# Attention queries and keys transposed in 32x32 blocks on VectorE during retention and placed through DRAM, instead of on TensorE during attention

## The chip, the cores and the metric

One Trainium2 chip, one of its cores. The metric is the device time of one execution in microseconds (us). The kernel before was run three times: 586.6, 587.24 and 587.29 us, median 587.24.

## What is computed

One layer of a trunk over 1,040 tokens (16 meta tokens and 1,024 others) of width 1,024, in fp32. A normalised input is projected once and cut into three groups: a gated short convolution, an attention with eight heads whose queries and keys come from small latents, and a retention with four heads. Their outputs are concatenated, projected and added to the input. The part that the change touches:

```python
q = (rms_norm(c_q, q_a_norm) @ w_uq).reshape(B, L, MLA_HEADS, QK_HEAD)      # 8 heads of 96 = 64 + 32
kv = (rms_norm(c_kv, kv_a_norm) @ w_ukv).reshape(B, L, MLA_HEADS, QK_NOPE + V_HEAD)
k = jnp.concatenate([k_nope, k_r], axis=-1)
q = rms_norm(q, q_norm)
k = rms_norm(k, k_norm)
q = jnp.concatenate([q[..., :QK_NOPE], apply_rope(q[..., QK_NOPE:], cos, sin)], axis=-1)
k = jnp.concatenate([k[..., :QK_NOPE], apply_rope(k[..., QK_NOPE:], cos, sin)], axis=-1)
s = jnp.einsum('bqhd,bkhd->bhqk', qb, k).astype(jnp.float32) * scale
s = jnp.where(mask[None, None], s, neg)          # blocks of 64 tokens, causal by block
p = jax.nn.softmax(s, axis=-1).astype(v.dtype)
return jnp.einsum('bhqk,bkhd->bqhd', p, v)
```

## The kernel before

Tokens are worked in eight tiles of 128 (`t` = 0 to 7) and one of the 16 meta tokens (`t` = 8). Nearly every matmul operand is kept as two parts, hi and lo, whose sum is the fp32 value, and a product is three matmuls (`mm3`, L112): hi with hi, hi with lo, lo with hi. `split` (L100 to L107) makes the parts: ScalarE rounds to hi, VectorE or GpSimd subtracts for lo.

The stages, in order:
- to about 60 us: inputs arrive; the gate of the attention group.
- to about 130 us: the attention's latents, queries, keys and values (`a_proj`, `a_lat`, `a_up`). Each token tile's queries and keys go to DRAM as q_s and k_s, tokens on rows (L368, L388).
- to about 256 us: retention, in two units `u` of two heads. For each token tile `r_proj` (L420) makes 24 matmuls; the steps behind it are put off by `later` and run one tile step on: `r_rope` rotates on VectorE (rt to qk, L441 to L444) and transposes on TensorE (L453); `r_score` makes the decayed product (qs, L472), `r_out` the output (rop, L487), `r_norm` and `fin` the rest (yp, L511).
- to about 355 us: the convolution, 128 channels at a time, cv, cz and cb being its matmul blocks. Its last quarter runs beside the first scores.
- to 540 us: the attention, head by head (`score`, `p_t`, `attend`), with the early part of the output projection (`partial`) as filling.
- the rest: the output projection.

`load_pair` (L535) reads k and q of a pair of heads back from DRAM, 128 tokens on the partitions. `qk_t` (L655) transposes them on TensorE, four blocks of 128x96 in a group, and splits the result out of PSUM into qT and kT, which the scores read; the weights of the query and key norm (wqk) are multiplied in at this split:

```python
def qk_t(h, g, which):                      # L655: head, half of the tokens, 0 = q, 1 = k
    tp = pst("tq", f"{'qk'[which]}Tp{h}_{g}")
    for j in range(4):
        nc.tensor.transpose(out=tp[:96, j * P:j * P + P], in_=src[:, 4 * g + j, cs], identity=ident)
    if which == 0:
        split(qT[h % 2][0][:96, gs], qT[h % 2][1][:96, gs], tp[:96], scale=wqk[:96])
    else:
        split(kT[h % 2][0][:96, gs], kT[h % 2][1][:96, gs], tp[:96])
```

A scheduler sets the order of each engine's instructions from the program and its own estimates; on the chip that order is fixed, and an engine that waits holds back all that stands behind. SP issues nearly all transfers, in one such queue. Buffers with one tag are shared in turn: hp_pool has two of tag "q" and two of tag "k", and the convolution's ccs, the retention's rwk and the keys share the latter. wp holds weights (12 pairs of hi and lo), wsp three staging tiles for them.

## Time and profile before

| | |
|---|---|
| median of 3 runs | 587.24 us |
| the profiled execution, first to last instruction | 590.4 us (its page gives no time beyond this span) |
| instructions | 9,705 |
| HBM read, written | 48.75 MB, 21.00 MB |
| busy: TensorE, VectorE, ScalarE, GpSimd | 98%, 56%, 42%, 38% |

How to read it: PE is TensorE, PEld its weight load, DVE VectorE, ACT ScalarE, POOL GpSimd, SP the engine that issues transfers. L661 is line 661 of the kernel. In a row `out<-in x8` names what is written, what is read and how many. Matmuls overlap, and the end of one is modelled, so durations of neighbours can't be added; starts can be compared. A row of the waits names who waited, for whom, how long in total, how often, and the longest.

### The profile page before, as it was taken

Reading aid. Unit: us, or ns where it says so; the run is one execution under the profiler, and the core shown is the slowest. Engines: PE = TensorE matmul, PEld = TensorE weight load, DVE = VectorE, ACT = ScalarE, POOL = GpSimd, SP = SyncE. Lnnn points to the kernel's source line nnn. Section 1 sums busy time; section 2 is a strip of 40 time slices with the busy share of each in tenths; the row PEclk is TensorE's granted clock in tenths of the full one; section 3 lists DMA queues with packets and bytes.
Section 4 is the critical chain, followed back from the end, with each engine's and each line's share of the span. In section 5 each row is a group of like instructions: output and inputs, shape, how many; then the busy total and the mean of one; then the engine's idle time right before and its main releaser. Section 6 shows DMA issues by size and latency. Waiting matters only on the chain.

```text
span 590.4 us, 9705 instructions
## 1 busy us (share of the span) xinstructions
PE 577.6 (98%) x3465; PEld 482.2 (82%) x3465; DVE 331.6 (56%) x777; ACT 249.3 (42%) x584; POOL 224.1 (38%) x327
## 2 busy tenths in 40 slices
PE   8989899999999999999999999999999999999996
PEld 5867799988777777788889888888888888877885
DVE  5547578888435442483252557766758658564132
ACT  6764445655114321341020327755656556544000
POOL 2023157677203230060430986634434344534000
PEclk9999899999999999999999999999999999999999
DMA  8787613364701300040102548316311223113086
GB/s 328 262 261 241 187 48 116 126 197 178 232 2 47 115 0 19 1 129 32 37 26 69 163 140 263 113 37 179 92 53 54 72 90 120 43 46 135 16 273 228
DMA packets 46656, 70.38 MB, mean 119 GB/s; under 512 B 3792, under 2 KB 21840, under 8 KB 46480
## 3 DMA queue, kind: packets, MB, share of 16 engines
q1 hardware_dynamic: 43008, 63.47, 33.5%
q10 hardware_dynamic: 3600, 6.29, 2.9%
q8 instruction: 27, 0.44, 0.3%
q14 instruction: 21, 0.17, 0.1%
HBM read 48.75 MB, written 21.00 MB: 118 GB/s over the span
## 4 chain that ended last, share of the span: by engine, by line
PE 84%; DMA 10%; DVE 3%; ACT 2%; issue 1%; SPq 0%; DVEq 0%; ACTq 0%
PE r L112 17%; PE S L112 9%; PE cv L112 8%; PE part L112 8%; PE A L112 6%; PE o L758 6%; PE pTp L717 5%; DMA out<-ot 4%; PE cz L112 4%; PE cb L112 4%; PE out L112 3%; PE qps L112 3%; DMA xs<-in_xT 2%; DMA xt<-in_x 2%; PE rsp L471 1%; DMA mz_s<-mzz 1%
## 5 line engine op out<-in xcount | busy, mean ns | idle before, releaser
L695 ACT ACTIVATE pr<-S,smx 128x144 f32<-128x144 f32 (+8 forms) x72 | 50.4, 701 | 27.2 <-DVE smx L686 13.3
L686 DVE TENSOR_REDUCE smx<-S 128x1 f32<-128x144 f32 (+8 forms) x72 | 49.8, 701 | 15.7 <-PE S L112 6.3
L703 POOL TENSOR_SCALAR pm<-pr,smx 128x16 f32<-128x16 f32 x64 | 18.5, 289 | 85.1 <-DVE smx L701 61.1
L704 POOL TENSOR_SCALAR pr<-pr,smx 128x128 f32<-128x128 f32 (+3 forms) x64 | 48.1, 752 | 0.6 <-DVE smx L701 0.6
L717 PE MATMUL pTp<-ident,pr 128*128 128x128 f32 x288 | 45.4, 274 | 0.0
L723 ACT COPY pt<-pTp 128x512 f32<-128x512 f32 (+2 forms) x64 | 31.8, 506 | 26.4 <-PE pTp L717 24.9
L717 PEld LDWEIGHTS pTp<-ident,pr 128*128 128x128 f32 x288 | 35.1, 140 | 5.3 <-issue 0.8
L448 POOL TENSOR_SCALAR kw<-qk,con 128x64 f32<-128x64 f32 (+1 forms) x36 | 14.4, 413 | 64.0 <-DVE qk L444 31.3
L758 PEld LDWEIGHTS o<-pt,v 128*64 128x64 f32 x448 | 26.6, 137 | 12.1 <-issue 4.8
L758 PE MATMUL o<-pt,v 128*64 128x256 f32 (+2 forms) x448 | 36.2, 309 | 0.0
L112 PE MATMUL r<-wh_r,xah 128*128 128x512 f32 (+1 forms) x80 | 30.3, 379 | 0.0
L112 PE MATMUL r<-wh_r,xal 128*128 128x512 f32 (+1 forms) x80 | 30.3, 378 | 0.0
L112 PE MATMUL part<-woh,yh 128*128 128x512 f32 x64 | 30.1, 471 | 0.0
L112 PE MATMUL r<-wl_r,xah 128*128 128x512 f32 (+1 forms) x80 | 30.0, 375 | 0.0
L875 DVE SCALAR_TENSOR_TENSOR ot<-out,xr 128x512 f32<-128x512 f32 (+1 forms) x17 | 11.2, 660 | 32.9 <-DMA out<-ot 17.6
L472 DVE TENSOR_TENSOR qs<-rsp,con 128x128 f32<-128x128 f32 x32 | 8.4, 288 | 31.9 <-PE rsp L471 31.8
L112 PE MATMUL r<-wh_r,xbl 128*128 128x512 f32 x64 | 26.1, 407 | 0.0
L112 PE MATMUL r<-wh_r,xbh 128*128 128x512 f32 x64 | 25.9, 405 | 0.0
L112 PE MATMUL r<-wl_r,xbh 128*128 128x512 f32 x64 | 25.7, 402 | 0.0
L112 PE MATMUL part<-wol,yh 128*128 128x512 f32 x64 | 25.5, 399 | 0.0
L112 PE MATMUL part<-woh,yl 128*128 128x512 f32 x64 | 25.2, 394 | 0.0
L766 DVE TENSOR_TENSOR ym<-o,ym 64x256 f32<-64x256 f32 x32 | 13.5, 420 | 16.7 <-PE o L760 16.2
(293 smaller groups left out, 1723.8 us busy)
## 6 DMA issues: line engine op xcount, KB each, us to landing
xt<-in_x SPq DMA_DIRECT2D x16, 256.0 KB, 4.3
ws_r<-in_win SPq DMA_DIRECT2D x16, 256.0 KB, 3.5
ws_c<-in_win SPq DMA_DIRECT2D x16, 256.0 KB, 3.0
wos<-in_wout SPq DMA_DIRECT2D x16, 256.0 KB, 3.5
xp<-in_x SPq DMA_DIRECT2D x16, 256.0 KB, 2.7
p_s<-xp SPq DMA_DIRECT2D x16, 256.0 KB, 2.0
xr<-p_s SPq DMA_DIRECT2D x15, 256.0 KB, 5.2
out<-ot ACTq DMA_DIRECT2D x15, 256.0 KB, 5.3
```

Of the source, the lines that this page charges most:

```text
L112: nc.tensor.matmul(out, lhsT=x_, rhs=y_, start=first and i == 0, stop=last and i == 2)
L448: nc.gpsimd.tensor_scalar(kw[R, j], qk[R, 2 + j], con[R, kd0 + j:kd0 + j + 1], 1.0, op0=ALU.mult, op1=ALU.mult)
L472: nc.vector.tensor_tensor(qs[:, 2 + j], sp[j][:, :P], DT[:, 2 * u + j], op=ALU.mult)
L686: nc.vector.tensor_reduce(sm[:, i // 2:i // 2 + 1], sp[:, :n, :w], axis=AX.XY, op=ALU.max, negate=True)
L695: e = nc.scalar.activation(pr[:, c0:c1].rearrange("p (b c) -> p b c", b=n), sp, AF.Exp, bias=mx, accum_out=sm[:, 5 + i:6 + i])
L703: nc.gpsimd.tensor_scalar(pm[(2 * h + t // 4) % 2][:, t % 4, :NM], pr[:, nk - NM:nk], sm[:, 9:10], 1.0, op0=ALU.mult, op1=ALU.mult)
L704: nc.gpsimd.tensor_scalar(pr[:, :nk - NM], pr[:, :nk - NM], sm[:, 9:10], 1.0, op0=ALU.mult, op1=ALU.mult)
L717: tr_ = nc.tensor.transpose(out=tp[:, b * P:b * P + P], in_=pr[:, c0:c0 + P], identity=ident)
L723: nc.scalar.copy(pt[:, b0:b0 + nb, tt], src)
L758: nc.tensor.matmul(op[64 * cg:64 * cg + 64, c0:c1], lhsT=lv, rhs=src[:, i_, c_], start=b == 0, stop=False)
L766: nc.vector.tensor_tensor(ys, op[64 * cg:64 * cg + 64, :256].rearrange("p (a c q) -> p a c q", a=2, q=64), ys, op=ALU.mult)
L875: nc.vector.scalar_tensor_tensor(ot, acc[:, c0:c1], 0.5, xt, op0=ALU.mult, op1=ALU.add)
```

## The change

- A new step, `turn`, runs eight times in the retention stage, one for each token-tile step from `u` = 0, `t` = 3 on: for each pair of heads first k, then q. It loads the pair's slice (ts) from k_s or q_s, multiplies the first 64 columns of each query by the norm weights (GpSimd, L527), transposes all 32x32 blocks on VectorE (L528, ts to td), and stores td to a new DRAM array T_s with four transfers of 32 partitions each, so that the array holds 96 rows a head and 1,024 tokens in a permuted order.
- `load_head` reads the 96x1,024 values of one head's k and q from T_s, for heads 0 and 1 after the third quarter of the convolution, later at the first tile of each head for the head after next.
- `qk_t` has no transpose: it splits what was loaded, through a view that undoes the permutation. The lo part of k is made on GpSimd now, that of q stays on VectorE.
- wqk becomes a row of 64 weights on all partitions.

```diff
+    def turn(hp, which):
+        src = hp_pool.tile([P, NT, 192], F32, tag="q", name=f"ts{hp}_{which}")
+        dst = hp_pool.tile([P, 6, NT * 32], F32, tag="q", name=f"td{hp}_{which}")
+        nc.sync.dma_start(src, (q_s, k_s)[which].rearrange("t p c -> p t c")[:, :, hp * 192:hp * 192 + 192])
+        if which == 0:
+            nope = src.rearrange("p t (h d) -> p (t h) d", h=2)[:, :, :64]
+            nc.gpsimd.tensor_tensor(nope, nope, wqk[:, None, :].to_broadcast([P, 2 * NT, 64]), op=ALU.mult)
+        nc.vector.transpose(dst.rearrange("p c (t k) -> p t c k", k=32), src.rearrange("p t (c k) -> p t c k", k=32))
+        to = T_s[which][hp].rearrange("(c f) (i r) -> i f c r", f=32, i=4)
+        for i in range(4):
+            nc.sync.dma_start(to[i], dst[32 * i:32 * i + 32])
+
+    turns = [(hp, w) for hp in range(4) for w in (1, 0)]
     for u in range(2):
         for t in [8] + list(range(NT)):
             r_proj(u, t)
             step()
+            if turns and t != 8 and (u or t >= 3):
+                turn(*turns.pop(0))
...
+    def load_head(h):
+        for which in (1, 0):
+            x = hp_pool.tile([P, 1536], F32, tag="qk"[which], name=f"{'qk'[which]}{h}")[:96, :SEQ]
+            nc.sync.dma_start(x, T_s[which][h // 2, 96 * (h % 2):96 * (h % 2) + 96])
+            raw[h, which] = x.rearrange("p (i t k) -> p t i k", i=4, k=32)
+
     def load_pair(hp):
-        qt = hp_pool.tile([P, NT, 192], F32, tag="q", name=f"q{hp}")
-        kt = hp_pool.tile([P, NT, 192], F32, tag="k", name=f"k{hp}")
...
-        nc.sync.dma_start(kt, k_s.rearrange("t p c -> p t c")[:, :, hp * 192:hp * 192 + 192])
-        nc.sync.dma_start(qt, q_s.rearrange("t p c -> p t c")[:, :, hp * 192:hp * 192 + 192])
...
         def qk_t(h, g, which):
...
-            for j in range(4):
-                nc.tensor.transpose(out=tp[:96, j * P:j * P + P], in_=src[:, 4 * g + j, cs], identity=ident)
-            if which == 0:
-                gs = slice(g * 512, g * 512 + 512)
-                split(qT[h % 2][0][:96, gs], qT[h % 2][1][:96, gs], tp[:96], scale=wqk[:96])
...
+            src = raw[h, which][:, 4 * g:4 * g + 4]
+            o = g * 512 + NM * which
+            dst = [x[:96, o:o + 512].rearrange("p (t i k) -> p t i k", i=4, k=32) for x in (qT, kT)[which][h % 2]]
...
+            split(*dst, src, lo_eng=nc.gpsimd if which else nc.vector)
...
+            if t == 0 and h + 2 < H:
+                load_head(h + 2)
```

The rows below are the orders of the two programs, without the number of each row (a number at the end of a name is a buffer's; the change's lines lie some 2 to 18 further down).

On SP, at the end of the queries and keys, before: the last store of q, one of the loads of v, the last store of k, the loads of the first two pairs' queries, then weights.

```order
L388 DMA q_s_70<-kqo7_1636 128x768
L541 DMA v1_3678<-v_s_72 128x8x128
L368 DMA k_s_71<-kqo7_1636 128x768
L540 DMA q0_3303<-q_s_70 128x8x192
L540 DMA q1_3676<-q_s_70 128x8x192
L118 DMA ws_r17_1930<-in_win 128x512
L118 DMA ws_c00_2471<-in_win 128x512
L118 DMA ws_c01_2477<-in_win 128x512
```

and now:

```order
L370 DMA k_s_71<-kqo7_1638 128x768
L523 DMA ts0_1_1890<-k_s_71 128x8x192
L531 DMA kT_s_74<-td0_1_1891 32x6x256 x4
L523 DMA ts0_0_2006<-q_s_70 128x8x192
L531 DMA qT_s_73<-td0_0_2007 32x6x256 x4
L523 DMA ts1_1_2082<-k_s_71 128x8x192
L531 DMA kT_s_74<-td1_1_2083 32x6x256 x4
L523 DMA ts1_0_2155<-q_s_70 128x8x192
L120 DMA ws_r17_1940<-in_win 128x512
L120 DMA ws_c00_2541<-in_win 128x512
L120 DMA ws_c01_2547<-in_win 128x512
L531 DMA qT_s_73<-td1_0_2156 32x6x256 x2
```

The two loads of queries gave way to turns: each is a load and four stores, and the weight loads r17, c00 and c01 stand behind the fourth turn's load.

On VectorE, around the rotation of tile 5 of the first retention unit (qk0_5), before:

```order
L472 TENSOR_TENSOR qs0_3_1884<-rsp0_3_0_1964,con_105 128x128
L472 TENSOR_TENSOR qs0_3_1884<-rsp0_3_1_1965,con_105 128x128
L482 SCALAR_TENSOR_TENSOR state0_1574<-state0_1574,con_105,rup0_3_1972 64x64 x2
L441 TENSOR_TENSOR qk0_5_2048<-rt0_5_2046,con_105 128x256
L442 TENSOR_TENSOR qk0_5_2048<-rt0_5_2046,con_105 128x4x32
L443 TENSOR_TENSOR qk0_5_2048<-rt0_5_2046,con_105 128x4x32
L460 SCALAR_TENSOR_TENSOR zsb0_4_1993<-zsb0_4_1993,rt0_5_2046 128x128
L444 TENSOR_TENSOR qk0_5_2048<-qk0_5_2048 128x256
L500 TENSOR_REDUCE so0_3_2026<-rwk0_3_2024 128x8
L501 SCALAR_TENSOR_TENSOR so0_3_2026<-so0_3_2026,con_105 128x8
```

and now:

```order
L474 TENSOR_TENSOR qs0_3_1886<-rsp0_3_1_1975,con_107 128x128
L446 TENSOR_TENSOR qk0_4_1989<-qk0_4_1989 128x256
L484 SCALAR_TENSOR_TENSOR state0_1576<-state0_1576,con_107,rup0_3_1982 64x64 x2
L528 STREAM_TRANSPOSE td1_1_2083<-ts1_1_2082 128x8x6x32
L443 TENSOR_TENSOR qk0_5_2067<-rt0_5_2065,con_107 128x256
L444 TENSOR_TENSOR qk0_5_2067<-rt0_5_2065,con_107 128x4x32
L445 TENSOR_TENSOR qk0_5_2067<-rt0_5_2065,con_107 128x4x32
L462 SCALAR_TENSOR_TENSOR zsb0_4_2003<-zsb0_4_2003,rt0_5_2065 128x128
L502 TENSOR_REDUCE so0_3_2045<-rwk0_3_2043 128x8
L446 TENSOR_TENSOR qk0_5_2067<-qk0_5_2067 128x256
L503 SCALAR_TENSOR_TENSOR so0_3_2045<-so0_3_2045,con_107 128x8
```

The third turn's transpose (td1_1) stands between the state of tile 3 and the rotation of tile 5; the rest is in the same order, except that a reduction of the norm (so0_3) comes ahead of the rotation's last addition.

On GpSimd, where the last quarter of the convolution meets the first heads (pm and pr are the normalisations of head 0's probabilities, wol the lo parts of output weights), before:

```order
L104 TENSOR_TENSOR wol7_0_3363<-wos7_0_3364,woh7_0_3362 128x512
L703 TENSOR_SCALAR pm0_3346<-pr0_0_3455,smx0_0_3449 128x16
L704 TENSOR_SCALAR pr0_0_3455<-pr0_0_3455,smx0_0_3449 128x128
L607 TENSOR_SCALAR wos6_1_3601<-wos6_1_3601,vec_76 128x512
L607 TENSOR_SCALAR wos7_1_3605<-wos7_1_3605,vec_76 128x512
L578 TENSOR_TENSOR yv1_1_3460<-yv1_1_3460,z1_1_3461 128x512
```

and now:

```order
L721 TENSOR_SCALAR pm0_3420<-pr0_0_3509,smx0_0_3503 128x16
L722 TENSOR_SCALAR pr0_0_3509<-pr0_0_3509,smx0_0_3503 128x128
L106 TENSOR_TENSOR wol7_0_3437<-wos7_0_3438,woh7_0_3436 128x512
L106 TENSOR_TENSOR kt1l_3399<-k1_3377,kt1h_3398 96x512 x2
L601 TENSOR_TENSOR yv1_1_3514<-yv1_1_3514,z1_1_3515 128x512
L721 TENSOR_SCALAR pm0_3420<-pr0_1_3556,smx0_1_3550 128x16
```

Two subtractions for the keys of head 1 (kt1l) stand ahead of the convolution's product and of the next normalisations; two for head 0 (kt0l) stand some ten rows earlier.

## Rows read from the trace of the kernel before

**Rows 1.** TensorE and the others, busy times of the page:

```profile
PE 577.6 (98%) x3465; PEld 482.2 (82%) x3465; DVE 331.6 (56%) x777; ACT 249.3 (42%) x584; POOL 224.1 (38%) x327
```

**Rows 2.** Waits of TensorE, longest first: who, for whom, total, times, longest:

```profile
PE A L112 <- ACT wh_A L103: 2.5, 1, 2.5
```

**Rows 3.** Windows: us, then busy PE, PEld, DVE, ACT, POOL, PEclk, DMA share, GB/s:

```profile
125.00:256.00 131.00, 131.00 (x698) 103.08 (x696) 65.82 (x197) 43.95 (x105) 42.48 (x58) 1.00 0.26 82
...
400.00:540.00 140.00, 139.95 (x1114) 116.74 (x1113) 92.63 (x226) 79.68 (x191) 62.26 (x109) 1.00 0.27 86
```

**Rows 4.** The tile of transposed keys: duration min/median/max ns, first and last start:

```profile
L661 PE MATMUL kTp<-ident,k x64: 270/272/274, 317.7 to 491.7; 128*96 128x128 f32 x64
```

**Rows 5.** Timeline of TensorE at a group of transposes: start us, us, what:

```profile
392.71 0.60 PE L661 MATMUL qTp<-ident,q 128*96 128x128 f32 x4
...
393.33 0.35 PE L112 MATMUL S<-kt0l,qt0h 104*128 104x400 f32 x1
393.51 0.35 PE L112 MATMUL S<-kt0h,qt0l 104*128 104x400 f32 x1
```

**Rows 6.** Loads of the slices k, then of q, from issue to landing, us:

```profile
DMA to landing us min/median/max: 4.7/5.9/7.1
...
DMA to landing us min/median/max: 6.2/6.5/8.3
```

**Rows 7.** Groups of GpSimd's instructions: busy us, mean ns | idle before:

```profile
L104 POOL TENSOR_TENSOR wol<-wos,woh 128x512 fp32r<-128x512 f32 x16 | 20.4, 1295 | 2.6 <-ACT woh L103 2.5
L703 POOL TENSOR_SCALAR pm<-pr,smx 128x16 f32<-128x16 f32 x64 | 18.5, 289 | 85.1 <-DVE smx L701 61.1
L704 POOL TENSOR_SCALAR pr<-pr,smx 128x128 f32<-128x128 f32 (+3 forms) x64 | 48.1, 752 | 0.6 <-DVE smx L701 0.6
```

**Rows 8.** VectorE's long rows, a group and two lines:

```profile
L104 DVE TENSOR_TENSOR yk<-ym,yq 128x1024 fp32r<-128x1024 f32 x2 | 2.4, 1210 | 0.0
...
L634 DVE CAST qt1h<-msk x1: 678/678/678, 330.9 to 330.9; 8x1024 fp32r<-8x1024 f32 x1
...
L635 DVE CAST kt1h<-msk x1: 1558/1558/1558, 333.0 to 333.0; 8x1044 fp32r<-8x1044 f32 x1
```

**Rows 9.** Timeline of SP's queue, the last store of k: start us, us:

```profile
151.49 0.32 SPq L368 DMA_DIRECT2D k_s<-kqo  x1
```

**Rows 10.** Transfers issued from 147 to 162 us: KB each, median us to landing:

```profile
k_s<-kqo SPq DMA_DIRECT2D x1, 384.0 KB, 3.5
```

**Rows 11.** Timeline of VectorE at the rotation of tile 5, start and end:

```profile
178.81 0.42 DVE L441 TENSOR_TENSOR qk<-rt,con 128x256 f32<-128x256 f32 x1 [3.93 <-ACT rt L435]
...
179.75 0.42 DVE L444 TENSOR_TENSOR qk<-qk 128x256 f32<-128x256 f32 x1
```

**Rows 12.** Timeline of TensorE, the transposes of that rotation:

```profile
184.40 0.38 PE L453 MATMUL rtp<-ident,qk 128*128 128x128 f32 x2
```

**Rows 13.** The projections r of the second unit, tiles 4 to 7:

```profile
L112 PE MATMUL r<-wh_r,xbh x32: 390/394/507, 225.2 to 254.6; 128*128 128x512 f32 x32
```

**Rows 14.** Windows after TensorE's wait for the first projection (columns as in rows 3):

```profile
60.00:62.00 2.00, 1.42 (x6) 1.23 (x7) 1.79 (x3) 1.30 (x3) 0.00 (x0) 0.69 0.87 285
62.00:64.00 2.00, 2.00 (x8) 1.90 (x7) 1.84 (x3) 1.35 (x3) 0.00 (x0) 0.50 0.92 286
```

**Rows 15.** Timeline of GpSimd before the clearing of vr [idle before <- releaser]:

```profile
346.71 0.70 POOL L703 TENSOR_SCALAR pm<-pr,smx 128x16 f32<-128x16 f32 x1 [1.38 <-DVE smx L701]
...
349.98 1.29 POOL L578 TENSOR_TENSOR yv<-yv,z 128x512 f32<-128x512 f32 x1 [0.86 <-DVE smx L701]
...
354.51 0.95 POOL L822 MEMSET vr<- 128x1024 f32 x1
```

**Rows 16.** Chain of TensorE from 348 to 355 us, the last convolution block:

```profile
348.64 5.51 PE cb L112 x24
```

**Rows 17.** Timeline of SP's queue, pieces of vr:

```profile
359.45 2.87 SPq L824 DMA_DIRECT2D vr<-v_s  x5
```

**Rows 18.** The tile vr: its pieces from issue to landing, us:

```profile
DMA to landing us min/median/max: 1.8/6.0/7.4
```

More of the change, by code (lines that the diff above doesn't have):

```diff
@@ L33 @@
 WTOT = _o
-V_LN, V_QA, V_KVA, V_QN, V_KN, V_CW, V_CB, V_RN = 0, 8, 10, 11, 12, 13, 19, 21
+V_LN, V_QA, V_KVA, V_CW, V_CB, V_RN = 0, 8, 10, 12, 18, 20
 NV = 22
@@ L77, in trunk @@
     v_s = dp.tile([L, 512], F32, name="v_s")
+    T_s = [dp.tile([4, 192, SEQ], F32, name=f"{c}T_s") for c in "qk"]
     mz_s = dp.tile([4, P, SEQ], F32, name="mz_s")
@@ L82, in trunk @@
     vec = cp.tile([P, NV], F32, name="vec")
-    wrow = cp.tile([P, 128], F32, name="wrow")
+    wrow = cp.tile([P, 256], F32, name="wrow")
     ident = cp.tile([P, P], F32, name="ident")
@@ L94, in trunk @@
     kml = cp.tile([96, H, NM], F32R, name="kml")
-    wqk = cp.tile([P, 1], F32, name="wqk")
+    wqk = cp.tile([P, 64], F32, name="wqk")
     def rsqrt(out, in_, n, rows=P):
@@ L594, in trunk @@
         conv_cb(u, g)
+    for h in range(2):
+        load_head(h)
     pairs = [load_pair(0)]
@@ L655, in qk_t @@
         def qk_t(h, g, which):
-            qt, kt, _ = pairs[h // 2]
-            cs = slice(96 * (h % 2), 96 * (h % 2) + 96)
-            tp = pst("tq", f"{'qk'[which]}Tp{h}_{g}")
-            src = (qt, kt)[which]
-            for j in range(4):
-                nc.tensor.transpose(out=tp[:96, j * P:j * P + P], in_=src[:, 4 * g + j, cs], identity=ident)
-            if which == 0:
-                gs = slice(g * 512, g * 512 + 512)
-                split(qT[h % 2][0][:96, gs], qT[h % 2][1][:96, gs], tp[:96], scale=wqk[:96])
-            else:
-                gs = slice(NM + g * 512, NM + g * 512 + 512)
+            src = raw[h, which][:, 4 * g:4 * g + 4]
+            o = g * 512 + NM * which
+            dst = [x[:96, o:o + 512].rearrange("p (t i k) -> p t i k", i=4, k=32) for x in (qT, kT)[which][h % 2]]
+            if which == 1:
                 if g == 0:
@@ L739, in attend @@
             nj = 4 * g + 4
-            pt, vt = pts.pop((h, g)), pairs[hp][2]
+            pt, vt = pts.pop((h, g)), pairs[hp]
             op = pst("o", f"o{h}_{g}")
@@ L964, in _layout @@
     sw = lambda v: np.concatenate([v[16:], v[:16]])
-    wrow = np.concatenate([qn[64:], sw(qn[64:]), kn[64:], sw(kn[64:])])
+    wrow = np.concatenate([qn[64:], sw(qn[64:]), kn[64:], sw(kn[64:]), qn[:64], kn[:64]])
     c, qm, km = _consts()
```

10 lines of the change are left out of this document (4 added, 6 removed).

## Prediction

> **What bounds the kernel now.** I read the busy times first: TensorE 98% of a span of 590.4 us, VectorE 56%, ScalarE 42%, GpSimd 38% [rows 1]. A share is an average, so the waits come next: the longest of TensorE is 2.5 us, for the first projection's weights at about 60 us [rows 2]. Then the windows by stage: in the retention stage it is busy 131.00 of 131.00 us, in the heads 139.95 of 140.00 [rows 3]. So TensorE is the bound from about 62 us to the end of the heads: what is taken off it comes off the time in full, and every wait that is put into its stream is paid in full. The sum is made against the profiled span, 590.4 us; the runs shown have a median of 587.24, 0.5% less, and I subtract from that median what the sum gives.
>
> **What TensorE loses.** The 128 transposes of L661 go, 64 of k [rows 4] and as many of q. The 0.27 us of such a row is a modelled duration, not a price, since matmuls overlap; the price is in the starts. A group of four starts at 392.71, the second score matmul behind it at 393.33: 0.62 us for four transposes and one matmul, and the next matmul of that kind takes 0.18 (393.33 to 393.51) [rows 5]. So a group costs 0.44 us, and 32 groups cost **14.1 us**.
> The Trainium skill (VectorE: DVE Perf Modes, The three transpose paths, and its Rules for kernel authors) gives 390 ns for a 128x128 transpose in bf16 on TensorE against 311 ns for blocks of 32 on VectorE, and advises TensorE for a full one where the output may go to PSUM, which speaks against this move. By its 390 ns the 128 would be worth 49.9 us, an estimate; the starts say 0.11 us each, and the rows decide.
>
> **What it adds in the retention stage.** Eight turns, one for each pair of heads and each of k and q. A turn is a chain: load of 768 KB, for q a multiplication of 1,024 columns on GpSimd, one transpose of 128x1536 on VectorE, four stores of 192 KB, and only then, on the same SP queue, the next turn's load. The transposes stand in the middle of VectorE's retention work, and what stands behind one waits with it.
> - Load: the same slices were read before, landing after 4.7 to 7.1 us (k) and 6.2 to 8.3 (q), medians 5.9 and 6.5 [rows 6]. In a turn, 768 KB of stores stand right before it; the q load that had another in front was the one of 8.3. I take L = 7.0, between.
> - Multiplication: 512 columns take 1.30 us on GpSimd [rows 7], so 1,024 take 2.6.
> - Transpose: no row shows one. 1,024 columns of fp32 take 1.21 us on VectorE, so 1,536 take **1.8 us**; the fastest row per column (1,024 in 0.68) gives 1.0, the slowest (1,044 in 1.56) 2.3 [rows 8].
> - Stores: four issues of 0.32 us on SP [rows 9], 1.3 us.
>
> A k turn is then 1.3 + L + 1.8 = 10.1 us, a q turn 12.7. The first load needs the last store of k: issued at 151.49 and landing 3.5 us later, 155.0 [rows 9, 10]; nothing stands before it, so it takes 5.9, and the first transpose ends at 162.7. The ends that follow are 175.4, 185.5, 198.2, 208.3, 221.0, 231.1 and 243.8 us.
> On SP the turns pass weight loads, r17, c00 and c01 behind the fourth turn's load. Each costs the queue an issue of some 0.3 us, and they now wait for the third turn's stores (about 187 us); r17 belongs to the second unit, whose projections start late enough to cover it.
>
> **Where TensorE meets that chain.** First behind the third transpose (185.5): the rotation of tile 5 stands behind it. Before, that rotation started at 178.81, its last part at 179.75 [rows 11], and TensorE took its transpose at 184.40 [rows 12]. Now its parts take 1.4 us (178.81 to 180.17) and the reduction between them 0.7 behind 185.5, to 187.6: **3.2 us** of waiting. The fourth to sixth transposes meet slack by the same reckoning. The seventh (231.1) stands ahead of the decay products of the second unit's tile 0, about 1.0 us later, 232.1. TensorE wants them after four matmuls of tile 4, whose projections began at 225.2 [rows 13]: 226 without waits, 229.1 with the first: **3.0 us** more. The eighth is covered. Together 6.2 us; as a rule for this order, the seventh ends at 189.1 + 6 L, so the waits are 6 L - 36 us, nothing below L = 6.0.
> A pause also costs clock: after the wait of 2.5 us [rows 2] the granted clock was 0.69 and 0.50 in two windows of 2 us [rows 14], so 0.6 + 1.0 = 1.6 us were lost, and a little in the next: 1.7. I charge this once, since what the first pause costs shortens the second; the bounds are none and twice.
>
> **Where TensorE meets GpSimd.** The low parts of k move from VectorE to GpSimd, 16 of 1.30 us [rows 7]. Heads 0 and 1 bring four, 5.2 us, into a stretch in which GpSimd is nearly full: ahead of the clearing of vr, which ends at 354.51 + 0.95 = 355.5, it is idle only 1.4 and 0.9 us [rows 15]. So that ends 3.0 us later, 358.5. Behind it stand three normalisations (0.29 + 0.75 each) and two weight parts of 1.30 [rows 7], 5.7 us: 364.2. The early output projection's second half wants those weights; on TensorE it now comes some 9 us (by the rows' own spacing) after the last convolution block, whose end is 348.64 + 5.51 [rows 16] less four groups of 0.44, 352.4: 361.4, a wait of 2.8. The fourth piece of vr was issued at 359.45 [rows 17] and lands up to 6.0 later [rows 18], 10 us after the clearing; now 368.5, wanted some 2.5 us behind those weights, 366.7: 1.8. Together **4.6 us**, between nothing and twice that.
> Of the rest, VectorE's low parts of q keep their length, ScalarE's rounding reads the same columns, and loads by head move the bytes that loads by pair moved; all lie beside TensorE's work, and if that cover is gone it is rival 3.
>
> **Sum:** -14.1 + 6.2 + 1.7 + 4.6 = -1.6 us: span 588.8, and from the median **585.6 us**. The likeliest case is that the move gives nearly all of its gain back, 581 to 590.
>
> **Rivals.**
> 1. The turns stay hidden (faster, **577.5 us**). If stores do not delay the load behind them, L is 5.9 to 6.2 and 6 L - 36 is at most 1.2; with GpSimd's waits of rows 15 to 18 a little smaller that is -14.1 + 4.4. For it: the medians of rows 6, and a store of 384 KB landed in 3.5 us among others [rows 10]. Against: the second of two loads took 8.3. With GpSimd hidden too, 573.
> 2. The turns pace the stage (slower, **593 us**). The place is the same VectorE queue; L = 8.3 in all turns [rows 6] makes the waits 13.8, and -14.1 + 13.8 + 1.7 + 4.6 = +6.0. It decides from L = 7.3, where waits of 7.8 just use up 14.1 - 6.3. For it: four stores right ahead of each load on one queue. Against: their issues already spread over 1.3 us. With transposes of 2.3 us as well, six of them add 3: 596, and 598 with more waiting on GpSimd.
> The Trainium skill (SBUF — State Buffer, Door 1: The DMA port swizzle) says that 32 partitions reach 8 of 16 ports and measured 189 GB/s there against 328 with 128. Each of these stores leaves from 32 partitions, so by it the four take 4.2 us, an estimate, and the load comes nearer to this rival. No run here shows such a store.
> 3. The change doesn't relieve TensorE where it is bound, because softmax and GpSimd then pace each head: only the eight groups of heads 0 and 1 are gained, 3.5 us, and with 12.5 us of waits it is **596 us**. Against it: VectorE was busy 92.6 and GpSimd 62.3 of 140 us in that stretch [rows 3], and the twelve low parts that GpSimd gets there are 15.6 us.
>
> **How the numbers follow.** Forecast 0.47, rival 1 0.25, rival 2 0.22, rival 3 0.06. A difference of 0.2%, 1.2 us, is about what can be told from none here. The forecast's own 581 to 590 splits into 0.18 faster, 0.16 same, 0.13 slower; with rival 1 faster is 0.43, same 0.16, slower 0.41. The range takes in both bounds, 574 (loads of 4.7, transposes of 1.0 and hardly a wait on GpSimd) to 598.
>
> **What would show it.** TensorE's matmuls fall by 128, and the starts of heads 2 to 5 come 1.8 us (four groups of 0.44) nearer to each other. In the retention stage TensorE shows waits on VectorE of about 3 us, at a transpose of tile 5 and at a product of the second unit's tile 0, and VectorE waits on the loads of ts or on GpSimd's product before each transpose. If these waits are nought, rival 1 holds; if L is over 8, rival 2. The forecast is wrong in its steps if a transpose of 128x1536 lies outside 1.0 to 2.3 us, if TensorE never waits for GpSimd's weights or vr between 350 and 375 us, or if heads keep their spacing.

## The result and the profile after

The changed kernel takes **605.91 us** (median of 4 runs, 605.21 to 606.78) against 586.92 of the kernel before in the same session (586.57 to 587.29): ratio 1.0336, 95% interval 1.0311 to 1.0361. It is 19 us slower; 585.6 was forecast, and the range ended at 598.

The page's busy times of the kernel after, against [rows 1]; TensorE has the 128 matmuls less that were foretold:

```profile
PE 574.3 (95%) x3337; PEld 472.3 (78%) x3337; DVE 339.5 (56%) x769; ACT 249.5 (41%) x584; POOL 257.1 (43%) x347
```

TensorE is busy for 3.3 us less, and idle for 29.2 us of its span instead of 12.8: the time is in waits. Those of TensorE after (who, line, for whom: total us, times, longest; S are the scores, pTp the transposes of the probabilities p), against [rows 2], where the longest was 2.5 and stood at 60 us:

```profile
PE S L114 <- ACT pr L713: 3.6, 1, 3.6
PE rop L489 <- DVE qs L474: 3.2, 3, 1.4
PE r L114 <- POOL wl_r L106: 3.0, 1, 3.0
...
PE yp L513 <- POOL rwk L508: 2.4, 1, 2.4
...
PE pTp L735 <- POOL pr L722: 2.2, 1, 2.2
...
PE rtp L455 <- DVE so L503: 1.4, 1, 1.4
```

rop, r, yp and rtp stand in the retention stage, 10.0 us together; S and pTp between the convolution and the first heads, 5.8 us. Windows of the kernel after say the same by stage, with the columns of [rows 3]: the retention stage, then a stretch of later heads.

```profile
122.80:267.50 144.70, 134.56 (x693) 104.07 (x692) 80.47 (x204) 43.98 (x105) 48.02 (x59) 0.98 0.56 157
400.00:540.00 140.00, 140.00 (x1029) 115.46 (x1028) 91.20 (x225) 82.96 (x201) 75.56 (x126) 1.00 0.27 86
```

In the first, TensorE is idle for 10.1 us where it was idle for none. In the second it is as busy as it was, and GpSimd has 13 us more to do.

The stages are cut at TensorE's own rows, in the list by form (min/mean/max ns, first and last start). Before, then after:

```profile
L112 PE MATMUL cb<-xbh,wl_c x16: 388/390/401, 301.2 to 353.7; 128*128 128x512 f32 x16
...
L112 PE MATMUL out<-woh,yq x34: 278/389/499, 540.2 to 583.6; 128*128 128x512 f32 x30, 128*128 128x256 f32 x4
```

```profile
L114 PE MATMUL r<-wh_r,xah x80: 276/394/628, 122.8 to 232.3; 128*128 128x512 f32 x64, 128*16 128x256 f32 x16
...
L114 PE MATMUL r<-wh_r,xbl x64: 390/398/628, 160.9 to 266.9; 128*128 128x512 f32 x64
...
L114 PE MATMUL cb<-xbh,wl_c x16: 388/392/397, 314.0 to 364.6; 128*128 128x512 f32 x16
...
L114 PE MATMUL out<-woh,yq x34: 281/389/497, 555.6 to 599.1; 128*128 128x512 f32 x30, 128*128 128x256 f32 x4
```

Between these starts (before's retention runs from 124.95 to 255.25; the last `out`, in another row, starts at 584.5 before and at 600.0 after), in us:

| stage, by TensorE's starts | before | after | change | forecast |
|---|---|---|---|---|
| retention: first r to last r | 130.3 | 144.1 | +13.8 | +7.9 |
| convolution: to the last cb | 98.5 | 97.7 | -0.8 | -1.8 |
| attention: to the first out | 186.5 | 190.9 | +4.4 | -7.7 |
| output: to the last out | 44.3 | 44.5 | +0.2 | 0 |

The sum is +17.6 us of the 19.0 between the medians; runs of one kernel differ by as much as the rest. (The two profiled spans, 590.4 and 603.5, differ by 13.1: what lies ahead of the first r and behind the last `out` took 4.5 us less in the profile after.)

### The profile page after: what moved, and what is told of

Its sections match the earlier page's. It is cut to its first block, busy times and chain, and to the rows that moved or that the text cites. A ratio compares the mean times of both kernels' runs of the same rounds, so it can differ in the third digit from the quotient of the medians.

```text
span 603.5 us, 9524 instructions
## 1 busy us (share of the span) xinstructions
PE 574.3 (95%) x3337; PEld 472.3 (78%) x3337; DVE 339.5 (56%) x769; ACT 249.5 (41%) x584; POOL 257.1 (43%) x347
## 4 chain that ended last, share of the span: by engine, by line
PE 60%; DVE 11%; DMA 11%; POOL 7%; issue 5%; SPq 2%; ACT 2%; POOLq 0%; DVEq 0%; ACTq 0%
PE S L114 9%; PE part L114 8%; PE out L114 7%; PE cv L114 7%; PE o L776 6%; PE pTp L735 5%; PE A L114 4%; PE cb L114 4%; PE cz L114 4%; DMA ts<-q_s 3%; DMA xt<-in_x 3%; DVE td L528 2%; DMA ts<-k_s 2%; POOL scq L100 2%; POOL ts L527 2%
## 5 line engine op out<-in xcount | busy, mean ns | idle before, releaser
L721 POOL TENSOR_SCALAR pm<-pr,smx 128x16 f32<-128x16 f32 x64 | 18.4, 288 | 66.5 <-DVE smx L719 53.3
L776 PE MATMUL o<-pt,v 128*64 128x256 f32 (+2 forms) x448 | 38.5, 311 | 0.0
L450 POOL TENSOR_SCALAR kw<-qk,con 128x64 f32<-128x64 f32 (+1 forms) x36 | 13.0, 375 | 58.0 <-DVE qk L446 30.2
L528 DVE STREAM_TRANSPOSE td<-ts 128x1536 f32<-128x1536 f32 x8 | 14.2, 1779 | 40.8 <-POOL ts L527 22.0
```

The source lines that it names most:

```text
L450: nc.gpsimd.tensor_scalar(kw[R, j], qk[R, 2 + j], con[R, kd0 + j:kd0 + j + 1], 1.0, op0=ALU.mult, op1=ALU.mult)
L528: nc.vector.transpose(dst.rearrange("p c (t k) -> p t c k", k=32), src.rearrange("p t (c k) -> p t c k", k=32))
L721: nc.gpsimd.tensor_scalar(pm[(2 * h + t // 4) % 2][:, t % 4, :NM], pr[:, nk - NM:nk], sm[:, 9:10], 1.0, op0=ALU.mult, op1=ALU.mult)
L776: nc.tensor.matmul(op[64 * cg:64 * cg + 64, c0:c1], lhsT=lv, rhs=src[:, i_, c_], start=b == 0, stop=False)
```

## The experiments

Two things failed at once, so the theories come in two sets. For the **retention stage**: the stores of a turn hold the SP queue longer than reckoned, and every load, transpose and TensorE step behind inherits that; the rivals are the load's own time, GpSimd's product, and the transposes themselves, which fill VectorE. For the **attention**: the low parts of k delay everything else on GpSimd between 340 and 376 us; the rivals are TensorE's order in the heads, and a group of transposes that was never worth 0.44 us. "Settled heads" are heads 2 to 5. Each kernel ran beside the kernel before, which took 586.9 to 588.7 us. Where a diff has a line only of before, that line was in the changed kernel.

**turns_alone and heads_alone: each half of the change by itself.** The first is the kernel before with the eight turns put in (the product multiplies by ones, and nobody reads T_s); the second is the changed kernel without them, its heads loading plain slices of q_s and k_s:

```
- turns = [(hp, w) for hp in range(4) for w in (1, 0)]
+ turns = []
- nc.sync.dma_start(x, T_s[which][h // 2, 96 * (h % 2):96 * (h % 2) + 96])
+ flat = (q_s, k_s)[which].rearrange("t p c -> (t p c)")[h * 96 * SEQ:(h + 1) * 96 * SEQ]
+ nc.sync.dma_start(x, flat.rearrange("(a b) -> a b", b=SEQ))
```

> Theory A (the loss has two parts that hardly touch each other: the turns cost the retention stage about 14 us of waits and clock, and taking the transposes off TensorE in the attention gains nothing): 587 + 14 = 601 us, with the same TensorE waits between 180 and 260 us as in the changed kernel (about 10 us in sum) and heads spaced as before. Rival B (the turns themselves are nearly hidden, and the time is lost where the attention now reads and splits its operands): 590 us or less.

> The turns are left out, and the heads read a slice of the same size of q_s or k_s, so that the scores are made of other numbers. Theory A: retention is as before, the heads lose about 1.2 us of the 1.8 us a head that the transposes took, and the transition from convolution to heads waits some 11 us with its clock: 587 + 4 = 591 us. Rival B, as above: 600 us or more. Rival C (the heads gain what the transposes took, once the retention stage is not disturbed): 573 to 578 us.

Measured: turns_alone 601.09 us, ratio 1.0235 (1.020 to 1.027); heads_alone 590.25, 1.0035 (1.0017 to 1.0054), both as theory A has them. The waits of TensorE in turns_alone are the four of the retention stage, rop and r first, and none behind it but 0.7 us in the convolution:

```profile
PE rop L488 <- DVE qs L473: 3.2, 3, 1.6
PE r L113 <- POOL wl_r L105: 2.9, 1, 2.9
```

In heads_alone they are those of the attention:

```profile
PE S L114 <- ACT pr L714: 3.8, 1, 3.8
PE pTp L736 <- POOL pr L723: 2.2, 1, 2.2
```

From the first r to the last out, turns_alone is 15.0 us longer than before and heads_alone 1.8: 16.8 of 17.6. So the halves hardly touch each other, and the half that takes 128 matmuls off TensorE is by itself no gain at all.

**one_store: the whole tile in one store.** The layout in DRAM is then another, so it gives the time alone; the bytes are the same.

```
- for i in range(4):
-     nc.sync.dma_start(to[i], dst[32 * i:32 * i + 32])
+ nc.sync.dma_start(…whole T_s[which][hp], 128 rows…, dst)
```

> The changed kernel with one store a turn in place of four (values land at other places of T_s, so the heads get other numbers). If the four issues, 2.3 us a turn where 1.3 were forecast, lengthen the turns: each turn is 1.5 us shorter, the seventh transpose 9 us sooner, the retention's waits of 10 us nearly gone: 596 to 599 us. Rival (the transposes stand too early in VectorE's order whatever the turn's length, since a shorter turn is also placed earlier): 602 us or more.

Measured: 592.75 us, 1.0085 (1.0055 to 1.0114), 13.2 below the changed kernel and better than expected. SP's queue in the kernel after (start us, us; four stores in a row), then in one_store:

```profile
173.06 2.31 SPq L531 DMA_DIRECT2D qT_s<-td  x4
175.48 0.81 SPq L523 DMA_DIRECT2D ts<-k_s  x1
```

```profile
169.71 0.32 SPq L530 DMA_DIRECT2D qT_s<-td  x1
170.13 0.37 SPq L523 DMA_DIRECT2D ts<-k_s  x1
```

Store and next load hold the queue for 3.2 us in the one, 0.8 in the other. The load lands in 6.2 us (median) instead of 6.9, the last transpose starts at 230.5 instead of 247.9, and the retention stage is 132.3 us long: 11.8 of the 13.2 us. Among VectorE's instructions five of the eight transposes stand where they stood, the others three or four places earlier, so it is not a better place that saves the time. Where the turns follow each other at once, four partial stores are what the stage could not hide. The Trainium skill (DMA: Bandwidth & Descriptors, Rules for kernel authors) advises one transfer of 128 partitions in place of two to its halves; these runs, with four quarters, agree, and give the price here: 2.4 us of queue a turn.

**ready_source: turns without load and product.** The transposes read a resident table of the same shape, so what they store has no use; VectorE and the stores have the same work.

```
- src = hp_pool.tile([P, NT, 192], F32, tag="q", name=f"ts{hp}_{which}")
+ src = con[:, :NT * 192].rearrange("p (t c) -> p t c", t=NT)
- nc.sync.dma_start(src, (q_s, k_s)[which]…)
- if which == 0: …the product on GpSimd…
```

> The changed kernel with turns that transpose a table that has long been in SBUF: loads of ts and the product are left out, the eight transposes and 32 stores stay, so that the heads get other numbers. Theory A (it is the wait for load and product that holds VectorE's queue, not the 14 us of transposes nor the stores): retention is as long as before, no wait of TensorE there over 1 us, 606 - 12 = 594 us. Rival (VectorE's work or the stores' traffic slows the stage): 601 us or more.

Measured: 596.34 us, 1.0128 (1.0095 to 1.0162). The retention stage is 3.5 us longer than before instead of 13.8. With nothing to wait for, the scheduler put the transposes earlier (141.9 to 173.0 us). At these places eight transposes and 32 stores cost a quarter of the loss, with one wait of 1.9 us and one of 1.0; the rest goes with the load and the product, but the places changed, too, so the run does not part the two.

**no_product: the turns without GpSimd's multiplication** (three lines taken out of the turn).

> The changed kernel without the multiplication of the queries by the norm weights on GpSimd in the four turns of q. Theory A says that this product, which waits for its load, holds GpSimd's queue (the low part of a weight of the second unit behind the fourth turn) and lengthens four of the eight turns by 2.4 us each: without it the wait of 3.0 us for that weight goes and the sixth and later transposes come 5 to 7 us sooner, so 606 - 6 = 600 us. Rival (load and stores alone pace the turns, the product lies beside them): 604 us or more.

Measured: 609.9 us, 1.037 (1.0339 to 1.0402): slower, a miss. With the product gone, the scheduler set the transposes earlier on VectorE, where they waited for their loads with TensorE behind them:

```profile
PE rop L489 <- DVE qs L474: 6.5, 2, 5.0
...
PE rtp L455 <- ACT rwk L514: 5.9, 1, 5.9
```

So it says nothing on GpSimd's price, and something on the method: an edit that changes the planner's costs changes the order, too.

**spaced: the same turns, each stretched over two steps of the pipeline.** The load goes out in one step, the product and the transpose are issued behind later instructions of the next, and the last two turns fall into the convolution. It computes everything.

```
- turn(*turns.pop(0))
+ turn(slot)   # even: transpose and store the last load, load the next; odd: product
+ with tc.issue_after(mark["v"]):
      nc.vector.transpose(…)
```

> The changed kernel with all of its work, but each turn spread over two tile steps: load, one step later the product behind GpSimd's decay of that step, two steps later the transpose behind the rotation of that step; six turns end in the retention stage, two in the convolution. Theory A (the place in the queues costs, not the work): the retention's waits of 10 us and their clock go but for 1 to 3 us, 606 - 11 = 595 us (593 to 598). Rival (loads, stores and transposes cost by themselves, wherever they stand): 602 us or more.

Measured: 595.04 us, 1.0128 (1.0097 to 1.016). The retention stage takes 129.8 us, about as before, with all four stores a turn left in place; one wait of 2.9 us stands in the convolution, where two turns now fall and which is 4.9 us longer than in the changed kernel. The loss of the retention stage is thus one of place, too: a transpose that stands where its load has landed costs TensorE nothing there.

**klo_vector and klo01: who computes the low parts of k.** The first puts all of them on VectorE, in the changed kernel; the second those of heads 0 and 1 alone, in heads_alone.

```
- split(*dst, src, lo_eng=nc.gpsimd if which else nc.vector)
+ split(*dst, src)                                                       # klo_vector
+ split(*dst, src, lo_eng=nc.gpsimd if which and h > 1 else nc.vector)   # klo01
```

> The changed kernel with the low part of k made on VectorE, as before the change. If GpSimd's low parts of 1.5 us stand ahead of the normalisations that TensorE's probability transposes wait for, the two waits of 2.2 and 3.6 us at the transition go and the heads come nearer to a gain of 1.8 us each: 606 - 12 = 594 us, 600 at most. Rival (the filler is gone: the score of the next tile and the softmax chain are what the small stalls wait for, whoever makes the low parts): 603 to 608 us.

> The heads without turns, with the low parts of k of heads 0 and 1 alone made on VectorE, those of the other heads on GpSimd. If GpSimd's backlog between convolution and heads (four low parts of 1.3 to 1.7 us) makes the two waits of 2.2 and 3.8 us there and the clock loss behind them, both go: 590 - 6 = 584 us (582 to 587). Rival (VectorE is as late with them, or the transition waits for something else): 588 to 592 us.

Measured: klo_vector 603.93 us, 1.0282 (1.0236 to 1.0327), hardly below the changed kernel. That is the rival's time, but not by its reason: the two waits of the attention fall to 0.8 us together, a wait of 2.7 for VectorE appears in the convolution, and the settled heads take 23.5 us again. klo01: 586.51 us, 0.9976 (0.9955 to 0.9996), as expected. Its waits where heads_alone had 3.8 and 2.2:

```profile
PE cz L114 <- DVE ccs L579: 2.5, 1, 2.5
...
PE S L114 <- ACT pr L714: 0.7, 1, 0.7
```

Four low parts moved back took 3.7 us off heads_alone, at a new wait of 2.5 us in the convolution. What filled GpSimd is in the next section.

**o_together and dummy: why the heads gain so little.** In the heads the order of TensorE changed, too: the o matmuls (128x64 in form), a block in the kernel before, are broken up. The timeline of TensorE (start us, us) before, then after:

```profile
432.38 3.10 PE L758 MATMUL o<-pt,v 128*64 128x256 f32 x36
435.26 0.44 PE L760 MATMUL o<-ptm,vr 128*64 128x128 f32 x4
```

```profile
453.50 1.37 PE L776 MATMUL o<-pt,v 128*64 128x256 f32 x20
454.80 0.33 PE L735 MATMUL pTp<-ident,pr 128*128 128x128 f32 x1
455.06 0.44 PE L778 MATMUL o<-ptm,vr 128*64 128x128 f32 x4
455.43 0.66 PE L735 MATMUL pTp<-ident,pr 128*128 128x128 f32 x4
```

o_together is heads_alone with each o block held behind the pending transposes of p, and the next transposes of p behind the block; dummy is heads_alone with four transposes of the identity put where each group of L661 stood, into the tile that the groups wrote:

```
+ with tc.issue_after(late.get("pe0", late["act"])):                   # o_together
+     p_t(h, t)
+ with tc.issue_after(late["pe"]):                                     # o_together
+     attend(seq[n - 1][0], seq[n - 1][1] // 4)
+ for j in range(4):                                                   # dummy
+     nc.tensor.transpose(out=tp[:, j * P:j * P + P], in_=ident, identity=ident)
```

> The heads without turns, as in the run of the heads alone (590.3 us), with one thing more: the output matmuls o of a half head are held behind the transposes of the probabilities that are issued with them, so that no transpose and no block of the early projection stands between the o of pt and the o of ptm. Theory D (TensorE does not wait in the heads; each change from the 64-row o matmuls to another kind and back costs 0.3 to 0.4 us of starts, and without the transposes of k and q the scheduler breaks each pair of o blocks three times, where before it broke none in heads 2 to 5): a head loses about 1.2 us, 590 - 7 = 583 us (581 to 585). Rival (the breaks cost nothing by themselves, they stand where TensorE would wait for softmax anyway): 588 to 592 us.

> The heads without turns as before (590.3 us), with four transposes of the identity on TensorE in each of the 32 groups in place of those of k and q, into the same PSUM tile, read by nobody. Theory F (in the heads TensorE has gaps of softmax and ScalarE's copies that such transposes fill, so that removing them gave back only about 0.8 of 1.8 us a head, and putting them in costs only as much): 590 + 6 = 596 us (593 to 599). Rival (they cost TensorE their full 14.1 us wherever they stand, and the time of the heads alone is lost elsewhere): 602 to 605 us.

Measured: o_together 594.11 us, 1.0104 (1.0078 to 1.013), above both of its ranges; dummy 600.05, 1.0217 (1.0187 to 1.0247), between the two ranges expected. By head, from the first transposed p of one to that of the next:

| us | before | after | heads_alone | klo01 | o_together | dummy |
|---|---|---|---|---|---|---|
| last cb to head 0 | 5.3 | 1.9 | 1.9 | 1.9 | 1.9 | 3.6 |
| heads 0 and 1 | 42.7 | 53.3 | 52.4 | 44.6 | 57.3 | 52.5 |
| heads 2 to 5, each | 23.54 | 22.95 | 22.96 | 22.95 | 22.21 | 24.73 |

The intervals do not hold quite the same matmuls. Heads 0 and 1 of the changed kernel hold 40 more of o and 6 fewer of S than before, together some 2 us by their starts; the last two heads hold 40 fewer of o and 12 more of S.

dummy prices the groups. The eight ahead of head 0 cost 3.8 us there (2.1 of it in the convolution). In heads 2 to 5 its 16 groups cost 1.77 us a head, 0.44 each, or 0.35 without 1.0 us of new short waits and six o that moved in. So the price was about right, and the heads of this order are 24.73 - 23.54 = 1.2 us longer than those of before with the same transposes in them, 0.8 without those waits and o. In heads 0 and 1 the eight groups cost 0.1 us: TensorE was waiting there in any case.

What makes the settled heads longer can be read from TensorE's starts. In heads 2 to 5 the o matmuls stand in 8 unbroken runs before, in 19 after and in 9 in o_together. From one o to the next it is 0.07 us and from one transpose of p to the next 0.11, but from a transpose to an o 0.24 and from an o to a transpose 0.22. A break by transposes thus costs some 0.28 us, and 11 more breaks some 3 us, 0.8 a head: an estimate from these starts. Heads 3 and 4 hold the same matmuls in all three kernels but for the 16 transposes of before, and take 23.5 us each before, 23.1 after and 22.4 in o_together, where 0.55 us a head is a new wait for p:

```profile
PE pTp L736 <- DVE ptm L752: 1.6, 3, 0.6
```

With that wait taken off, an estimate, a head would gain 1.7 of the 1.8 us. But o_together paid 4.9 us in heads 0 and 1, where TensorE waited for ScalarE's p (5.4 us; 3.8 in heads_alone), for its copies (1.1) and for a weight's low part (1.0). The Trainium skill (TensorEngine Tiling (Array Packing), Key Properties) says that a change of tiling drains TensorE, which would make each break of a 64-column block cost something. The trace agrees: the one transpose between two pieces of o takes 0.26 us of starts (454.80 to 455.06), each of the four in a row behind them 0.14 (455.43 to 456.00, where the scores start). But no run changed the breaks and nothing else.

**The causes undone together.** store1_klo01 is the full computation with one store a turn and klo01's edit. T_s then keeps VectorE's blocks, and a head's slice comes back in three loads:

```
- T_s = [dp.tile([4, 192, SEQ], F32, name=f"{c}T_s") for c in "qk"]
+ T_s = [dp.tile([4, 6, P, 256], F32, name=f"{c}T_s") for c in "qk"]
- (four stores of 32 partitions)
+ nc.sync.dma_start(T_s[which][hp].rearrange("c p r -> p c r"), dst)
+ for c in range(3):
+     nc.sync.dma_start(x[32 * c:32 * c + 32].rearrange("f (i r) -> f i r", i=4), T_s[…][…, 3 * (h % 2) + c]…)
+ split(*dst, src, lo_eng=nc.gpsimd if which and h > 1 else nc.vector)
```

> The changed kernel with one store a turn (T_s laid out so that a turn is one transfer, and a head's slice three) and the low parts of k of heads 0 and 1 on VectorE; it computes all of the layer. If the two causes add up (one store: 13.2 us of 605.9; low parts: 3.7 us of the heads alone): 592.8 - 3.7 = 589 us (587 to 591), just above the kernel before. Rival (the heads' three transfers a slice, or the turns' different place, cost again): 592 us or more.

Measured: 589.36 us (587.1 to 590.98), 1.0026 (1.0005 to 1.0047), as expected: the ratio of 1.0336 has come down to 1.0026, and the retention stage is 132.9 us long. The store is issued in 0.36 us and the next load in 0.5:

```profile
169.92 0.36 SPq L529 DMA_DIRECT2D qT_s<-td  x1
170.38 0.48 SPq L523 DMA_DIRECT2D ts<-k_s  x1
```

It writes pieces of 1 KB, as the four did, so it was not the pieces that held the queue, but four issues from 32 partitions each. Of these the first takes 0.3 us, as a store alone does, the next two 0.44 and the last 0.99 in most turns; whether four stores of all partitions would do the same was not run. Two waits are left:

```profile
PE cz L114 <- DVE ccs L578: 2.6, 1, 2.6
PE rtp L455 <- ACT rwk L514: 2.6, 1, 2.6
```

**Four attempts at more.** spaced_klo01 and spaced_klo0 are spaced with the product moved to VectorE, into the split of q, and with the low parts of heads 0 and 1, or of head 0 alone, on VectorE. store1_klo01_o holds the o blocks behind the pending transposes from head 2 on. store1_klo01_m holds head 1's splits behind the convolution's multiplication for which cz waited.

> The spaced turns (595.0 us), the low parts of k of heads 0 and 1 on VectorE (which took 3.7 us from the heads alone), and the norm weights multiplied into the loaded queries on VectorE, a half head at a time, in place of GpSimd's product in the turns. If the causes add up: 595 - 4 - 2 = 589 us (586 to 591), about the time of the kernel before. Rival (VectorE becomes late at the transition with the product and the low parts): 594 us or more.

> As the run before it, but only head 0 has its low parts of k on VectorE, head 1 on GpSimd again. If the remaining wait at the transition is VectorE's (the convolution's product behind k's and q's low parts) this splits the load and takes 1 to 2 us more off: 587 to 588 us. If GpSimd's backlog decides, it is 1 to 3 us slower than with both heads on VectorE.

> As the run before it, with the output matmuls o held behind the transposes of the probabilities from head 2 on, so that their blocks are whole; in the heads alone this took a head of the steady state from 22.96 to 22.21 us and lost its gain at the first heads. If the broken blocks are what keeps the heads from gaining the transposes' 1.8 us: 589 - 5 * 0.74 = 585 us (584 to 587), and a head of 22.2 us. Rival (held blocks make TensorE wait for ScalarE's copies): 589 us or more.

> The kernel of one store a turn and low parts of k of heads 0 and 1 on VectorE (589.4 us), with head 1's splits held behind the convolution's last multiplication of its first half on VectorE. If the wait of 2.6 us that TensorE still has there, with a granted clock of 0.97 over 55 us (1.6 us), comes from VectorE's splits of head 1 standing ahead of that multiplication, each of them stretched beside GpSimd: 589 - 4 = 585 us (584 to 587), a little below the kernel before. Rival (the convolution's multiplication waits for something else, or head 1's scores are then late): 588 to 591 us.

All four missed: 598.47 us (ratio 1.0189, 1.0159 to 1.0219), 603.92 (1.028, 1.0253 to 1.0307), 598.1 (1.016, 1.0124 to 1.0197) and 594.78 (1.0137, 1.0104 to 1.0169). The two of which the waits tell most: in store1_klo01_m the wait at cz is gone and the last cb comes 2.4 us earlier, but the first head takes 28.6 us instead of 22.2 and the settled heads 23.4. In the two spaced ones S waits 7.6 and 10.5 us for ScalarE. No kernel of this study that computes the layer beats the one before: klo01 is 0.2% below it, its interval ending just under 1, but its heads read slices that are not transposed.

## Why the prediction was wrong

The stages of the table missed their forecasts by 5.9 us in retention, 1.0 in the convolution, 12.1 in the attention and 0.2 in the output, 19.2 of the 20.3 us between 605.9 and 585.6. With the groups at 0.44 us where they stood, the attention's 12.1 are 9.5 in heads 0 and 1 and 4.6 in the settled heads, less 2.0 around them.

**Right in its parts.** A transpose takes 1.78 us (1.8 foretold), the product 2.4 (2.6), the load 6.9 in the median (7.0), the matmuls fall by 128, and TensorE meets the chain on VectorE and on GpSimd, though not where I said. VectorE's transposes and GpSimd's products after (min/median/max ns, first and last start), and the loads' time to landing:

```profile
L528 DVE STREAM_TRANSPOSE td<-ts x8: 1778/1779/1779, 158.1 to 247.9; 128x1536 f32<-128x1536 f32 x8
...
L527 POOL TENSOR_TENSOR ts<-ts,wqk x4: 2357/2377/2405, 168.9 to 245.5; 128x1024 f32<-128x1024 f32 x4
...
DMA to landing us min/median/max: 4.7/6.9/7.4
```

**First failed step: "four issues of 0.32 us on SP, 1.3 us".** That was [rows 9], the issue of a store of 128 partitions that stands alone. Four in a row from 32 take 2.3 us, and the load behind them is issued in 0.83 instead of 0.37 (a part of its 6.9 us to landing):

```profile
L531 SPq DMA_DIRECT2D kT_s<-td x16: 302/440/990, 159.9 to 237.3; - x16
```

From the end of a transpose to the issue of the next load it took 2.4 to 2.5 us in five of the six turns before the seventh, and 3.6 in the fourth, among whose stores one of y_s stands, where I had 1.3. So the seventh transpose ended 7 us later than in my list once the clocks of the two profiles are set alike (their stages start 2.1 us apart). one_store shows the size: with this one term changed the stage is 11.8 us shorter and the kernel 13.2. My rule "the waits are 6 L - 36" left the stores' own time out of the range: rival 2 let L alone grow, though its place, VectorE's queue, was the right one.

**In the same stage: the meeting places.** Of the 10.0 us of waits only 2.8 stand at the two places that I named: 1.4 at the rotation of tile 5 (rtp, 3.2 foretold) and 1.4 at the second unit's first decay product (rop, 3.0 foretold). The other 7.2 stand behind turns that I had called covered: r behind the fourth product (3.0), rop behind the fifth transpose (1.3), yp behind the sixth (2.4), rop behind the eighth (0.5). The rule 6 L - 36 counts the first two places alone.

One of them is a queue that the list left out. I followed the turns past the weight loads on SP ("r17, c00 and c01") and not the product's place on GpSimd. The product of the fourth turn waits for its load, and behind it stands the low part of another weight of the second unit, r15, for which TensorE then waits. GpSimd, then TensorE (in brackets the idle time before, and what ended it):

```profile
194.01 2.36 POOL L527 TENSOR_TENSOR ts<-ts,wqk 128x1024 f32<-128x1024 f32 x1 [3.47 <-issue]
196.33 1.27 POOL L106 TENSOR_TENSOR wl_r<-ws_r,wh_r 128x512 fp32r<-128x512 f32 x1
```

```profile
197.66 0.29 PE L114 MATMUL r<-wl_r,xah 128*16 128x256 f32 x1 [3.02 <-POOL wl_r L106]
```

Before, TensorE did not wait for that low part:

```profile
188.05 1.30 POOL L104 TENSOR_TENSOR wl_r<-ws_r,wh_r 128x512 fp32r<-128x512 f32 x1 [3.12 <-ACT wh_r L103]
```

Nor was r17 covered, as I had it: its load was issued at 191.5 instead of 187.7, and its low part, on VectorE behind the fourth transpose, started at 198.1. Had r15 been ready, TensorE would have come to r17 at about 195 and waited for that instead, an estimate from the starts of its matmuls. The waits of the stage came to 10.0 us in place of 6.2, and the clock to 3.4 in place of 1.7: the granted clock was 0.92, 0.91 and 0.83 in these windows of 10 us, with the wait for the weight in the first.

```profile
190.00:200.00 10.00, 6.97 (x48) 4.73 (x47) 6.20 (x12) 2.51 (x5) 4.72 (x5) 0.92 0.50 155
200.00:210.00 10.00, 10.00 (x48) 7.74 (x49) 3.74 (x13) 1.64 (x5) 0.61 (x2) 0.91 0.87 249
...
230.00:240.00 10.00, 7.17 (x31) 5.11 (x31) 5.28 (x11) 1.76 (x4) 1.99 (x3) 0.83 0.54 146
```

**Right engine, wrong step and half the size: "where TensorE meets GpSimd", 4.6 us.** It cost 5.8 us of waits and some 3.2 of clock while TensorE worked, summed over windows of 2 us: just inside the bound of twice that. The low parts took 1.5 us each in the mean, where I had 1.30, but what came too late was not the weights or vr, for which TensorE never waited there: the prediction had named that as a sign of a wrong step. It was a normalisation of p (2.2 us) and a step that I had not followed, the convolution's product yv, both behind the low parts of k. ScalarE's next exponential waits 6.0 us for yv by the profile, and the scores wait for that exponential. GpSimd, ScalarE and TensorE after:

```profile
363.56 2.98 POOL L106 TENSOR_TENSOR kt1l<-k,kt1h 96x512 fp32r<-96x512 f32 x2
...
371.05 1.27 POOL L602 TENSOR_TENSOR yv<-yv,rb 128x512 f32<-128x512 f32 x1
```

```profile
372.35 0.70 ACT L713 ACTIVATE pr<-S,smx 128x528 f32<-128x528 f32 x1 [6.03 <-POOL yv L602]
```

```profile
373.19 0.70 PE L114 MATMUL S<-kt0h,qt0h 104*128 104x392 f32 x1 [3.56 <-ACT pr L713]
```

Before, that product began 1.0 us ahead of the start of the last cb (353.74); here it begins 6.4 behind it (364.62):

```profile
352.76 1.30 POOL L579 TENSOR_TENSOR yv<-yv,rb 128x512 f32<-128x512 f32 x1
```

klo01 shows the cause: with four low parts elsewhere, the first two heads take 44.6 us instead of 52.4. The granted clock is 0.95 and 0.53 in these windows. It falls while TensorE waits (from 366.7 to 373.2 but for 0.7 us) and is 0.50, the lower of its two levels, from 370 to 378:

```profile
360.00:370.00 10.00, 7.40 (x37) 5.81 (x35) 6.41 (x11) 2.29 (x6) 10.00 (x12) 0.95 0.54 163
370.00:380.00 10.00, 6.81 (x19) 5.88 (x20) 2.16 (x5) 4.04 (x10) 8.98 (x14) 0.53 0.49 161
```

**Second failed step: "a group costs 0.44 us, and 32 groups cost 14.1 us".** The price held roughly (dummy: 0.35 to 0.48). "What is taken off it comes off the time in full" did not, although TensorE is as busy in the heads as it was. The eight groups ahead of head 0 came back in full. Eight groups lay in heads 0 and 1, where TensorE then waited. And in the settled heads the scheduler, with these transposes gone, breaks the o matmuls into 19 runs instead of 8, which makes a head 0.8 to 1.2 us longer: it gained 0.6 us instead of 1.8. I had taken the order of what stays for given, and a share of 100% for a bound that only the count of matmuls moves. Rival 3 foretold heads that gain nothing, but for another reason (softmax or GpSimd as the bound); no wait is listed there, so that reason did not occur.

**The sum as it came:** in the heads -3.4 (head 0 starts earlier behind the last cb), +10.6 (heads 0 and 1, some 2 of it work that was elsewhere before), -2.4 (four settled heads) and -0.4 behind them, +4.4 us; in the retention stage +13.8; with -0.8 and +0.2, +17.6.

**What stays open:** whether whole o blocks can be had without the waits that came with them. Two kernels held the blocks together and got 0.75 and 0.5 us a head, with 0.5 and 0.8 us a head of new waits, and both lost more at the first heads. That the breaks cost the settled heads their gain is read from starts and from o_together; no run isolates a break, or shows whether it is TensorE's draining that costs.

## What to carry to other kernels

Count a transfer by what it holds its queue for, and by how many it is cut into: four partial stores and the load behind them took 3.2 us of queue where one store and the load took 0.8, and every step of an in-order chain behind paid it. Put a step that waits for a load where the load has landed, on every engine that it uses, and list what stands behind it on each. What is taken off the bounding engine comes back only as far as the order of what stays is kept, so compare the order of whole blocks, and the fill of the engine that took the work over, before counting the gain.

## What the runs showed of the hardware that was not expected

VectorE's low part of k can take five times as long beside GpSimd. Of two rows in klo01 the short one lies beside a clearing on GpSimd, the long one beside casts and two low parts of weights; VectorE, then GpSimd:

```profile
327.22 0.68 DVE L106 TENSOR_TENSOR kt0l<-k,kt0h 96x512 fp32r<-96x512 f32 x1
...
332.44 3.60 DVE L106 TENSOR_TENSOR kt0l<-k,kt0h 96x512 fp32r<-96x512 f32 x1
```

```profile
332.84 2.54 POOL L106 TENSOR_TENSOR wol<-wos,woh 128x512 fp32r<-128x512 f32 x2
```

In the kernel before, where the transposed k came from PSUM, all eight rows of that tile took 0.68 us, also the first, which lies beside such a low part of GpSimd:

```profile
L104 DVE TENSOR_TENSOR kt0l<-kTp,kt0h x8: 675/682/687, 335.7 to 469.1; 96x512 fp32r<-96x512 f32 x8
```

The Trainium skill (SBUF — State Buffer, SBUF: two separate sides) says that an operation of VectorE with two inputs in SBUF and one of GpSimd that reads SBUF shut each other out for a whole instruction. The rows agree: from 332.44 to the end of GpSimd's low parts are 2.9 us, and 0.68 more make 3.6; the clearing has no input. No run isolated it. It bears on this change, since q and k now come from DRAM into SBUF, where the transposes had left them in PSUM.
